# Feed-forward products of a four-layer trunk: each 128-row product issued as two 64-row products into two PSUM banks

## The chip, the cores and the metric

One core of a Trainium2 chip runs the whole program. The metric is device time in microseconds (us), median over runs. The kernel before was run twice: 3420.98 and 3409.43 us, median 3415.2 us. TensorE's clock has two levels, 1.2 and 2.4 GHz; the profile's granted clock is a share of the upper one (1.00 is 2.4 GHz).

## The reference, cut to what matters

256 latent tokens and 256 context tokens, 1024 channels, four layers. Each layer has a mixer (even layers: RWKV-7 time mixing and neighbourhood attention; odd layers: gated DeltaNet and an S5 state space model), an output projection, and a SwiGLU channel mixer with 2816 hidden channels, which is the part that changes:

```python
def swiglu(h, w_gate, w_up, w_down):
    return (jax.nn.silu(h @ w_gate) * (h @ w_up)) @ w_down

h_lat = h_lat + m_l[5] * swiglu(modulate(rmsnorm(h_lat, norm_ffn[l]), m_l[3], m_l[4]), f_gate[l], f_up[l], f_down[l])
if ctx_out:      # all layers but the last: the context tokens too
    h_ctx = h_ctx + m_c[5] * swiglu(...)
```

## The kernel before

Activations are channel-major: a tile `hT` of [128 partitions, 8 channel tiles, 512 tokens]. Every large fp32 product is made of three fp32r products, since both operands are split into a high and a low part: wh·xh, wh·xl, wl·xh (lines 222, 223 and 224 of `gemm`).

`unit` brings a piece of a weight matrix, 512 columns of 128 partitions (256 KB): a DMA on SP's queue (line 187, tile `w`, three buffers), a cast on ScalarE into `wh` (line 190) and a subtraction on VectorE into `wl` (line 191); `wh` and `wl` have three buffers each. In the feed-forward part a unit holds two channel tiles k of 256 output columns, so it feeds 2 x 2 x 3 = 12 matmuls. `gemm` takes 256 output columns at a time, in two PSUM banks, one for each 128 columns; the bank pairs alternate between tags "g" (tiles `pg` and `ph`) and "b" (two `pb` tiles), so one pair fills while the other is read.

`ffn` (line 355) first makes the modulated norm `nh`, `nl` (`norm_mod`, lines 322 to 326), channel tile by channel tile. It then runs over hidden blocks of 6, 6, 6 and 4 column tiles. For two column tiles at a time it computes the gate (`gate`: ScalarE reads the bank through Silu, line 370, into `sg`) and the up product (`up`: VectorE multiplies bank and `sg`, line 376; ScalarE and VectorE split the result into `gh` and `gl`, lines 377 and 378). After a block, the down product over its 6 or 4 channel tiles is added to `hT` (`add_h`, line 335, one VectorE instruction for each half of 256 tokens and each bank). Layers 0 to 2 work on 512 tokens, layer 3 on the 256 latent ones. In layers 0 and 2 `step()` also prepares the weights of the next S5 model (tiles whose names begin with `s5`), mostly on VectorE; these are the lines 1442 to 1640.

The program is written as Python code, but a scheduler sets the order on each engine, by a timeline that it models itself. Each engine then runs its own fixed order, and waits at an instruction until what it needs is there. So how many S5 instructions VectorE has to get through before a given `wl` is a matter of that order.

## Time and profile before

| what | value |
|---|---|
| median of the two runs | 3415.2 us (3409.43 to 3420.98) |
| span of the profiled execution | 3398.9 us |
| TensorE matmuls (PE) busy | 3120.2 us, 92% |
| weight loads (PEld) busy | 2418.1 us, 71% |
| VectorE (DVE) busy | 1920.1 us, 56% |
| ScalarE (ACT) busy | 1291.6 us, 38% |
| the four feed-forward stretches, together | 1351 us of the span |

PE stands for TensorE's matmuls, PEld for its weight loads, DVE for VectorE, ACT for ScalarE and SP for the queue that issues DMAs. The ends of matmuls are modelled, so the pace of matmuls is read from the distance of their starts, not from their durations. L222 is line 222 of the kernel. A group of instructions is written out<-in with the tiles' names, and the number in brackets behind a wait is its length with the one that ended it.

### The profile page before, as it was taken

Reading aid. Unit: us, or ns where it says so; the run is one execution under the profiler, and the core shown is the slowest. Engines: PE = TensorE matmul, PEld = TensorE weight load, DVE = VectorE, ACT = ScalarE, POOL = GpSimd, SP = SyncE. Lnnn points to the kernel's source line nnn. Section 1 sums busy time; section 2 is a strip of 40 time slices with the busy share of each in tenths; the row PEclk is TensorE's granted clock in tenths of the full one; section 3 lists DMA queues with packets and bytes.
Section 4 is the critical chain, followed back from the end, with each engine's and each line's share of the span. In section 5 each row is a group of like instructions: output and inputs, shape, how many; then the busy total and the mean of one; then the engine's idle time right before and its main releaser. Section 6 shows DMA issues by size and latency. Waiting matters only on the chain. (4 is left out here: it accounts for less than half of the span.)

```text
span 3398.9 us, 63286 instructions
## 1 busy us (share of the span) xinstructions
PE 3120.2 (92%) x24452; PEld 2418.1 (71%) x24452; DVE 1920.1 (56%) x4229; ACT 1291.6 (38%) x2785; POOL 515.4 (15%) x1159
## 2 busy tenths in 40 slices
PE   7999789999999889899999998877999999977998
PEld 4876456787787667578887776545787777756997
DVE  3556545766436696343434556555676445685554
ACT  3334344332235335232223333434333224534444
POOL 0223310000001653000000123220000000563000
PEclk8998889999999899899998998889999999978999
DMA  8635655345345544733336634553334334644554
GB/s 282 178 97 130 151 141 156 87 136 143 111 125 143 167 126 144 245 119 94 96 100 191 184 103 128 126 125 101 102 127 136 111 113 145 196 156 156 160 176 134
DMA packets 549696, 479.21 MB, mean 141 GB/s; under 512 B 176533, under 2 KB 480531, under 8 KB 549395
## 3 DMA queue, kind: packets, MB, share of 16 engines
q1 hardware_dynamic: 549394, 475.17, 48.5%
q8 instruction: 193, 3.16, 0.4%
q14 instruction: 109, 0.89, 0.1%
HBM read 406.34 MB, written 72.90 MB: 141 GB/s over the span
## 5 line engine op out<-in xcount | busy, mean ns | idle before, releaser
L191 DVE TENSOR_TENSOR wl<-w,wh 128x512 fp32r<-128x512 f32 x786 | 545.8, 697 | 766.4 <-ACT wh L190 746.6
L190 ACT CAST wh<-w 128x512 fp32r<-128x512 f32 x786 | 484.5, 619 | 1159.7 <-PE pb L223 343.3
L222 PE MATMUL pg<-nh,wh 128*128 128x512 f32 (+2 forms) x760 | 294.6, 388 | 19.4 <-ACT nh L270 8.7
L222 PE MATMUL pb<-nh,wh 128*128 128x512 f32 (+1 forms) x832 | 305.3, 374 | 4.0 <-ACT nh L325 2.7
L223 PE MATMUL pb<-nl,wh 128*128 128x512 f32 (+1 forms) x832 | 306.5, 371 | 0.0
L224 PE MATMUL pb<-nh,wl 128*128 128x512 f32 (+1 forms) x832 | 299.8, 373 | 0.0
L223 PE MATMUL pg<-nl,wh 128*128 128x512 f32 (+2 forms) x760 | 291.4, 383 | 0.6 <-DVE gr L1179 0.6
L224 PE MATMUL pg<-nh,wl 128*128 128x512 f32 (+2 forms) x760 | 290.4, 382 | 0.1
L298 POOL TENSOR_TENSOR nr<-nv,cst_base 128x4 f32<-128x4 f32 (+1 forms) x9 | 8.4, 938 | 1660.8 <-DVE nv L296 1660.8
L222 PE MATMUL ph<-nh,wh 128*128 128x512 f32 (+1 forms) x624 | 242.0, 388 | 10.1 <-ACT nh L325 5.9
L224 PE MATMUL ph<-nh,wl 128*128 128x512 f32 (+1 forms) x624 | 240.1, 385 | 0.0
L223 PE MATMUL ph<-nl,wh 128*128 128x512 f32 (+1 forms) x624 | 239.5, 384 | 0.0
L165 PE MATMUL px<-mw,cnd 128*32 128x256 f32 x1536 | 158.8, 450 | 83.5 <-DMA mw<-in_mod_w_dram 68.9
L222 PEld LDWEIGHTS pg<-nh,wh 128*128 128x128 f32 (+1 forms) x760 | 146.3, 193 | 56.4 <-ACT nh L270 11.3
L222 PEld LDWEIGHTS pb<-nh,wh 128*128 128x128 f32 x832 | 158.6, 192 | 36.3 <-ACT nh L325 3.2
L223 PEld LDWEIGHTS pb<-nl,wh 128*128 128x128 f32 x832 | 159.5, 192 | 29.3 <-DVE nl L271 1.3
L224 PEld LDWEIGHTS pb<-nh,wl 128*128 128x128 f32 x832 | 155.5, 191 | 30.7 <-issue 1.0
L223 PEld LDWEIGHTS pg<-nl,wh 128*128 128x128 f32 (+1 forms) x760 | 146.1, 192 | 34.8 <-issue 3.0
L224 PEld LDWEIGHTS pg<-nh,wl 128*128 128x128 f32 (+1 forms) x760 | 145.7, 192 | 29.1 <-issue 1.0
L858 POOL TENSOR_TENSOR Etmp<-E 64x14 f32<-64x14 f32 (+13 forms) x448 | 160.6, 359 | 31.1
L860 POOL TENSOR_TENSOR E<-E,Etmp 64x14 f32<-64x14 f32 (+13 forms) x448 | 158.8, 354 | 32.9
L222 PEld LDWEIGHTS ph<-nh,wh 128*128 128x128 f32 x624 | 119.6, 192 | 39.7 <-ACT nh L325 6.7
(578 smaller groups left out, 6440.8 us busy)
## 6 DMA issues: line engine op xcount, KB each, us to landing
mw<-in_mod_w_dram SPq DMA_DIRECT2D x192, 512.0 KB
w<-in_f_gate_dram SPq DMA_DIRECT2D x176, 256.0 KB
w<-in_f_up_dram SPq DMA_DIRECT2D x176, 256.0 KB
w<-in_f_down_dram SPq DMA_DIRECT2D x176, 256.0 KB
w<-in_w_in_even_dram SPq DMA_DIRECT2D x104, 256.0 KB
w<-in_w_in_odd_dram SPq DMA_DIRECT2D x80, 256.0 KB
w<-in_w_out_dram SPq DMA_DIRECT2D x64, 256.0 KB
hd<-hT SPq DMA_DIRECT2D x32, 256.0 KB
```

The lines of the kernel that those rows point to most:

```text
L165: nc.tensor.matmul(p[32 * c:32 * c + 32, :256], self.cnd[:, k, :], wt[:, 256 * c:256 * c + 256], start=k == 0, stop=k == KT - 1, skip_grou ...
L190: nc.scalar.copy(wh[:, :n], w[:, :n])
L191: nc.vector.tensor_tensor(wl[:, :n], w[:, :n], wh[:, :n].bitcast(F32), op=ALU.subtract)
L222: nc.tensor.matmul(o, wh[:, kk, m:m + mm], xh[:, k, tok], start=i == 0, stop=False)
L223: nc.tensor.matmul(o, wh[:, kk, m:m + mm], xl[:, k, tok], start=False, stop=False)
L224: nc.tensor.matmul(o, wl[:, kk, m:m + mm], xh[:, k, tok], start=False, stop=i == kt - 1)
L298: nc.gpsimd.tensor_tensor(r, v, self.mhalf[:, :nt], op=ALU.pow)
L858: nc.gpsimd.tensor_tensor(o, E[:, :s, s:s + 1].to_broadcast([m8, s, v]), E[:, s:s + 1, s + 1:].to_broadcast([m8, s, v]), op=ALU.mult)
L860: nc.gpsimd.tensor_tensor(E[:, :s, s + 1:], E[:, :s, s + 1:], o, op=ALU.add)
```

## The change

Each product of the feed-forward part is issued as two matmuls, one over partitions 0 to 63 and one over partitions 64 to 127, each into a PSUM bank of its own; whoever reads the result adds the two banks. `gemm_rows` takes 128 output columns at a time, in a pair of banks, and a unit of weights holds four channel tiles of 128 columns instead of two of 256. The gate now takes a copy on ScalarE, an addition on VectorE and the Silu on ScalarE; the up product takes a copy on ScalarE, an addition and a multiplication on VectorE before the split; `add_h` runs twice for each column tile.

```diff
+    def gemm_rows(self, W, kt, c0, cols, xh, xl, tok, done):
+        nc = self.nc
+        nt = tok.stop - tok.start
+        halves = (slice(0, 64), slice(64, 128))
+        ku = UNIT // 128
+        for m in range(cols // 128):
+            self.ngemm += 1
+            tag = "gb"[self.ngemm % 2]
+            ps = [self.bank(tag)[:, :nt] for _ in halves]
+            for k0 in range(0, kt, ku):
+                kn = min(ku, kt - k0)
+                wh, wl = self.unit(W[:, k0:k0 + kn, c0 + 128 * m:c0 + 128 * m + 128], kn, 128)
+                for kk in range(kn):
+                    k = k0 + kk
+                    for i, (w, x) in enumerate(((wh, xh), (wh, xl), (wl, xh))):
+                        for r, p in zip(halves, ps):
+                            nc.tensor.matmul(p, w[r, kk, :], x[r, k, tok], start=k == 0 and i == 0,
+                                             stop=k == kt - 1 and i == 2)
+            done(m, *ps)
...
-                def gate(m, p):
+                def gate(m, p, q):
                     s = fp.tile([128, NT], F32, name="sg", bufs=3)[:, :n]
-                    nc.scalar.activation(s, p, AF.Silu)
+                    nc.scalar.copy(s, p)
+                    nc.vector.tensor_tensor(s, s, q, op=ALU.add)
+                    nc.scalar.activation(s, s, AF.Silu)
                     gs.append(s)
 
-                def up(m, p):
+                def up(m, p, q):
                     s = gs[m]
                     i = 2 * u + m
-                    nc.vector.tensor_tensor(s, s, p, op=ALU.mult)
+                    t = self.tmp.tile([128, NT], F32, name="nt")[:, :n]
+                    nc.scalar.copy(t, p)
+                    nc.vector.tensor_tensor(t, t, q, op=ALU.add)
+                    nc.vector.tensor_tensor(s, s, t, op=ALU.mult)
                     nc.scalar.copy(gh[:, i, tok], s)
                     nc.vector.tensor_tensor(gl[:, i, tok], s, gh[:, i, tok].bitcast(F32), op=ALU.subtract)
...
-                self.gemm(Wg, KT, c0, 256, nh, nl, tok, gate)
-                self.gemm(Wu, KT, c0, 256, nh, nl, tok, up)
+                self.gemm_rows(Wg, KT, c0, 256, nh, nl, tok, gate)
+                self.gemm_rows(Wu, KT, c0, 256, nh, nl, tok, up)
                 step()
-            self.gemm(Wd[:, b0:b0 + nb, :], nb, 0, D, gh, gl, tok, lambda k, p: self.add_h(l, 40, k, p, tok))
+
+            def down(k, p, q):
+                self.add_h(l, 40, k, p, tok)
+                self.add_h(l, 40, k, q, tok)
+            self.gemm_rows(Wd[:, b0:b0 + nb, :], nb, 0, D, gh, gl, tok, down)
```

Line numbers of the changed kernel: the two matmuls stand on line 247, gate on 393 to 395, up on 402 to 406, `add_h` on 358; lines from 250 on have moved by 23, those behind `ffn` by 32 (L1606 of the change is L1574 of before).

The scheduler's order moves at more places than the diff shows. On TensorE, at the start of layer 0's feed-forward part, before (names: `pb` banks, `nh` and `nl` operands, `s5ct` an S5 transpose):

```order
L222 MATMUL pb<-nh,wh 128x512 x2
L1546 MATMUL pf<-cst_base,s5ct 128x128
L223 MATMUL pb<-nl,wh 128x512
L224 MATMUL pb<-nh,wl 128x512
L223 MATMUL pb<-nl,wh 128x512
L224 MATMUL pb<-nh,wl 128x512
L222 MATMUL pb<-nh,wh 128x512 x2
```

The same place of the change:

```order
L247 MATMUL pb<-nh,wh 128x512 x2
L247 MATMUL ph<-nh,wh 128x512
L247 MATMUL pg<-nh,wh 128x512
L1578 MATMUL pf<-cst_base,s5ct 128x128
L247 MATMUL pb<-nl,wh 128x512 x2
L247 MATMUL pb<-nh,wl 128x512 x2
L247 MATMUL pb<-nh,wh 128x512 x2
L247 MATMUL ph<-nl,wh 128x512
L247 MATMUL pg<-nl,wh 128x512
L247 MATMUL ph<-nh,wl 128x512
L247 MATMUL pg<-nh,wl 128x512
```

Every product is now a pair with the same operands and two banks (`pb` twice, or `ph` and `pg`), and two column tiles are begun side by side. Of the 6336 pairs 6256 stand side by side, and at 81 places something other than a pair stands between two of them.

On VectorE, later in the same part of layer 0, where the chain of the S5 powers ends with L1574 (L1606 of the change). Before, the last eleven rows up to it and the `wl` behind it:

```order
L191 TENSOR_TENSOR wl<-w,wh 128x512
L1572 TENSOR_TENSOR s5X<-s5t_7013,s5t_7014 128x32
L1567 TENSOR_TENSOR s5t_7013<-s5X 128x32
L1568 TENSOR_TENSOR s5t_7014<-s5X 128x32
L1569 TENSOR_TENSOR s5X<-s5t_7013,s5t_7014 128x32
L1570 TENSOR_TENSOR s5t_7013<-s5X 128x32
L1571 TENSOR_TENSOR s5t_7014<-s5X 128x32
L1573 COPY s5X<-s5X 128x8x32
L1572 TENSOR_TENSOR s5X<-s5t_7013,s5t_7014 128x32
L1574 TENSOR_SCALAR s5X<-s5X 128x8x32
L191 TENSOR_TENSOR wl<-w,wh 128x512
```

The change, around the same instruction:

```order
L1604 TENSOR_TENSOR s5X<-s5t_7123,s5t_7124 128x32
L1599 TENSOR_TENSOR s5t_7123<-s5X 128x32
L1600 TENSOR_TENSOR s5t_7124<-s5X 128x32
L1601 TENSOR_TENSOR s5X<-s5t_7123,s5t_7124 128x32
L1602 TENSOR_TENSOR s5t_7123<-s5X 128x32
L1603 TENSOR_TENSOR s5t_7124<-s5X 128x32
L1605 COPY s5X<-s5X 128x8x32
L1604 TENSOR_TENSOR s5X<-s5t_7123,s5t_7124 128x32
L1606 TENSOR_SCALAR s5X<-s5X 128x8x32
L191 TENSOR_TENSOR wl<-w,wh 128x512
L1615 TENSOR_TENSOR s5X<-s5cc,s5pout 128x576
L1618 TENSOR_TENSOR s5X<-s5cc,s5pout 128x576
```

The chain is the same; what has moved is the subtractions L191. Counted from the last `nl` of the norm, 19 of them stand ahead of L1574 before, with 149 S5 instructions; in the change 4 stand ahead of L1606, with 144 S5 instructions and two additions of the gate, and the L191 in the rows above is the fifth behind the last `nl` and the sixth of the layer. In layer 2 the order is the same.

On ScalarE, in the steady part (names: `sg` the gate, `nt` the copy of the first bank), before:

```order
L370 ACTIVATE sg<-pg 128x512
L190 CAST wh<-w 128x512
L370 ACTIVATE sg<-ph 128x512
L190 CAST wh<-w 128x512 x4
L377 CAST gh<-sg 128x512 x2
L190 CAST wh<-w 128x512 x3
```

and in the change:

```order
L190 CAST wh<-w 128x512 x2
L393 COPY sg<-pb 128x512
L395 ACTIVATE sg<-sg 128x512
L190 CAST wh<-w 128x512 x2
L402 COPY nt<-pg 128x512
L405 CAST gh<-sg 128x512
L190 CAST wh<-w 128x512 x2
```

Two casts of weights alternate with the two instructions that read a column tile, and the second of these waits for VectorE's additions in between.

## Rows read from the trace of the kernel before

**Rows 1.** The page: span, and busy time of each engine.
```profile
span 3398.9 us, 63286 instructions
PE 3120.2 (92%) x24452; PEld 2418.1 (71%) x24452; DVE 1920.1 (56%) x4229; ACT 1291.6 (38%) x2785; POOL 515.4 (15%) x1159
```
**Rows 2.** Busy time by stretch, the four feed-forward parts, layers 0 to 3.
```profile
core 0: us, PE busy (x) PEld busy (x) DVE busy (x) ACT busy (x) POOL busy (x), PEclk, DMA share, GB/s
630.00:1015.00 385.00, 383.86 (x1929) 308.14 (x1927) 229.56 (x494) 122.00 (x214) 0.00 (x0) 1.00 0.42 125
1450.00:1828.00 378.00, 378.00 (x1679) 302.40 (x1677) 148.68 (x254) 112.55 (x191) 0.00 (x0) 1.00 0.35 107
2438.00:2820.00 382.00, 381.28 (x1917) 305.97 (x1916) 225.48 (x480) 120.82 (x212) 0.00 (x0) 1.00 0.42 124
3178.00:3384.00 206.00, 199.42 (x1605) 193.00 (x1604) 119.25 (x216) 98.42 (x188) 0.00 (x0) 0.98 0.54 162
```
**Rows 3.** Timeline, gate and up of layer 1: start us, us, engine, line, instruction.
```profile
1509.54 0.39 PE L223 MATMUL pb<-nl,wh 128*128 128x512 f32 x1
1509.54 0.19 PEld L224 LDWEIGHTS pb<-nh,wl 128*128 128x128 f32 x1
...
1516.77 0.40 PE L224 MATMUL pb<-nh,wl 128*128 128x512 f32 x1
```
**Rows 4.** Timeline, TensorE, down of layer 1.
```profile
1517.70 0.39 PE L222 MATMUL ph<-gh,wh 128*128 128x512 f32 x1
...
1522.24 0.39 PE L224 MATMUL ph<-gh,wl 128*128 128x512 f32 x1
```
**Rows 5.** Timeline, TensorE: L674's 64-row pairs and what follows; L1609's full ones.
```profile
120.04 0.50 PE L674 MATMUL pf<-ar,bk 64*128 64x128 f32 x6
120.60 0.39 PE L674 MATMUL pf<-ar,bk 64*128 64x128 f32 x4
120.92 0.39 PE L244 MATMUL pg<-wl,nh 128*128 128x256 f32 x1
...
679.15 0.60 PE L1609 MATMUL pf<-cst_base,s5wt 128*128 128x128 f32 x4
```
**Rows 6.** Single lines: count, duration ns min/median/max, first and last start.
```profile
L376 DVE TENSOR_TENSOR sg<-sg,pb x44: 676/687/690, 1471.7 to 2791.9; 128x512 f32<-128x512 f32 x44
L370 ACT ACTIVATE sg<-pg x22: 597/598/602, 1462.2 to 2780.0; 128x512 f32<-128x512 f32 x22
L335 DVE SCALAR_TENSOR_TENSOR hT<-pb,mod,hT x140: 471/476/485, 577.4 to 3379.5; 128x256 f32<-128x256 f32 x140
L376 DVE TENSOR_TENSOR sg<-sg,pg x11: 410/413/415, 3191.6 to 3366.9; 128x256 f32<-128x256 f32 x11
L370 ACT ACTIVATE sg<-pb x22: 377/378/387, 3186.6 to 3361.4; 128x256 f32<-128x256 f32 x22
```
**Rows 7.** Last nl of layer 0's norm, and L1574's starts.
```profile
635.45 0.48 DVE L326 SCALAR_TENSOR_TENSOR nl<-nt,mod,nh 128x256 fp32r<-128x256 f32 x1
...
L1574 DVE TENSOR_SCALAR s5X<-s5X x2: 286/290/295, 688.9 to 2495.0; 128x256 f32<-128x256 f32 x2
```
**Rows 8.** Busy time between the two: all engines; VectorE's on wl; VectorE's on sg.
```profile
635.93:689.20 53.27, 53.27 (x238) 42.82 (x237) 47.85 (x176) 19.65 (x35) 0.00 (x0) 1.00 0.36 108
...
635.93:689.20 53.27, 13.05 (x19) 1.00 0.36 108
...
635.93:689.20 53.27, 5.21 (x8) 1.00 0.36 108
```
**Rows 9.** TensorE during that norm: us, busy (count), clock, DMA.
```profile
619.00:635.93 16.93, 15.77 (x61) 0.82 0.22 55
```
**Rows 10.** Layer 3: one unit's DMA, its cast, ScalarE's waits (total, times, longest).
```profile
3242.04 0.37 SPq L187 DMA_DIRECT2D w<-in_f_gate_dram  x1
...
3245.05 0.62 ACT L190 CAST wh<-w 128x512 fp32r<-128x512 f32 x1 [0.44 <-DMA w<-in_f_gate_dram]
...
ACT wh L190 <- DMA w<-in_f_up_dram: 25.4, 26, 2.1
```

## The prediction

> **What bounds the kernel now.** The page comes first: TensorE's matmuls are busy for 92% of the span, VectorE for 56%, ScalarE for 38% [rows 1]. Shares are means over unlike stages, so the second view is busy time by stretch, for the four feed-forward parts alone [rows 2]: in layers 0 to 2 TensorE is busy 383.86 of 385.00, 378.00 of 378.00 and 381.28 of 382.00 us at a granted clock of 1.00. There is no idle time for a reader or a load to give back; the only thing to gain is the pace of the products, and whatever holds TensorE up is added in full. VectorE has 149 of 378 us in layer 1 but 230 and 225 in layers 0 and 2, where the S5 preparation adds 81 and 77 us. Layer 3 has TensorE at 199.42 of 206.00 us.
>
> The third view is the timeline, for the pace. In gate and up 31 products lie between the two starts, 1509.54 and 1516.77: 233 ns each [rows 3]; in down 20 lie between 1517.70 and 1522.24: 227 ns [rows 4]. If a column takes one clock at 2.4 GHz, which is my estimate and fits these rows, 512 columns are 213 ns, and 14 to 20 ns a product are something else. Each weight load starts with the product ahead of it and takes 0.19 us [rows 3]: it is hidden already.
>
> **The change, part by part.** The sum is made against the profiled span, 3398.9 us; the median of the runs shown is 16.3 us above it, and I add that at the end.
>
> *Pace of the pairs.* The feed-forward parts hold 4 x 3 x 528 = 6336 products (22 x 8 each for gate, up and down, three matmuls each), 4752 of 512 columns and 1584 of 256. Each becomes a pair over the two halves of the partitions. The nearest rows are the pairs of L674, also 64 rows and 128 output columns into two banks, though plain fp32 and 128 columns wide: the pair at 120.04 and that at 120.60 are five pairs apart, 112 ns a pair [rows 5]. Full products of the same type and width, L1609, take (0.60 - 0.27) / 3 = 109 ns each, 0.27 being the modelled length of the last [rows 5]. So a pair costs what one costs, and 3 ns: 6336 x 3 = 19 us. Bounds: no pair beats its streaming, which for the 512-column ones is (231 - 213) x 4752 = 86 us of gain, and about 104 with the narrow ones at 118 against 107 ns (118 is an estimate: half of 233 is 117, and layer 3's 199.42 us over 1605 matmuls, waits included, are 124 [rows 2]); above, two products one behind the other, which is a rival.
>
> *Changes of form on TensorE.* At 81 places something else stands between two pairs. In the rows the last pair of L674 starts at 120.60 + 0.112 = 120.71 and the full product behind it at 120.92 [rows 5], 0.21 us later, 0.09 more than a pair's own step. In and out, at 81 places, that is 15 us; S5 products of narrow shape paid some of it before. I take 10, with 0 and 20 as ends.
>
> *The order on VectorE at the start of layers 0 and 2.* This is the largest term, and the diff does not show it. The last `nl` of layer 0's norm ends at 635.93 and L1574 ends at 689.2 [rows 7]. Between them VectorE works 47.85 us, 13.05 of it on nineteen L191 and 5.21 on the gate's readers [rows 8], so 47.85 - 13.05 - 5.21 = 29.6 us are 149 S5 instructions. In the change 144 of these stand ahead of the sixth `wl` of the layer, with four L191 and two additions between. The five left out are some of 0.7 us each, so 29.6 - 3.5 + 6 x 0.69 = 30 us have to pass on VectorE behind the last `nl` before the sixth `wl` is even begun, or 31 when it is done (an L191 takes 13.05 / 19 = 0.69 [rows 8], an addition out of a bank as much [rows 6]). Until then TensorE can finish five units, 60 pairs. Before, it had done about 55 products by the end of the norm (61 matmuls in that stretch, a few of them S5 transposes [rows 9]) and does 31 / 0.233 = 133 more in the next 31 us. The change is behind by 188 - 62 = 126 products, or 29 us; a part of the 81 us of S5 work on VectorE is then done earlier, but TensorE never had room to regain it. I take 28 for each of the two layers, 56 together; from 14 (if the chain is run through in half the time) to 35 (if the two additions, which wait for their tile's products, hold the queue, and the idle stretches bring the slow clock that the norm shows with 0.82 [rows 9]).
>
> *The readers in layers 0 to 2.* Gate: a copy of 0.60, an addition of 0.69 and a Silu of 0.60 us in the place of a Silu; up: a copy and an addition more; down: two L335 of 0.48 us more for each column tile [rows 6]. On VectorE that is 44 x 0.69 + 32 x 2 x 0.476 = 61 us a layer, and 12 further loads of weights (the six channel tiles of a down block need two units for 128 columns, 16 in the place of 12 units for a block) 8 us: layer 0 has 299 of 385 us, layer 1 218. A column tile is 24 pairs, 5.6 us, and its banks must be free one tile later; the chain copy, addition, multiplication, two L191 takes 0.60 + 2 x 0.69 + 2 x 0.69 = 3.4 us. It is covered by the other pair of banks, and costs nothing as long as it is. What is left uncovered is the tail of a block, where down waits for the last up tile's longer chain, 0.60 + 0.69 = 1.3 us more, at twelve blocks of these layers: 15 us at most. I take 10; from 0 to 40, if some tiles also lose their cover.
>
> *Layer 3.* Here a tile lasts only 24 x 0.118 = 2.8 us. A unit's cast starts 3.01 us after its DMA is issued [rows 10]; with the cast of 0.62 and an L191 of 0.69 [rows 8] a buffer of three goes round in 4.3 us, 1.44 a unit, against 12 x 0.118 = 1.42 for TensorE: ScalarE already waits for these DMAs, 25.4 us for one of the three matrices alone [rows 10]. The change puts into ScalarE's queue, behind every two casts, a copy and a Silu or split with VectorE's additions between: 0.38 + 0.41 + 0.38 = 1.2 us for gate, 1.6 for up [rows 6]. Two tiles then need a round of the buffer, a cast and this gap, 4.3 + 0.62 + 1.2 to 1.6, so 3.05 to 3.25 us a tile: 44 x 0.3 = 13 us. In down a tile of six channel tiles takes 18 x 0.118 = 2.1 us but two units, near 2.7 us: 24 x 0.6 = 14 us. I take 25, from 0 (the loads run ahead) to 50. The same bytes arrive in runs half as long; one round longer by 0.3 us would add 6 us, inside that range.
>
> *Sum.* 19 + 10 + 56 + 10 + 25 = 120 us: 3398.9 + 120 + 16.3 = 3535 us. The order in the three later mixers changes too, with the same work; I have no row for it, take 0, and leave 20 us to both sides.
>
> **The rivals.** *The pairs do not overlap.* The rows that show overlap are plain fp32, and at 112 ns for 128 columns they stream at half the rate of the fp32r products (233 ns for 512) [rows 3, 5]. If fp32r halves ran one behind the other, the cost would be 4752 x 0.231 + 1584 x 0.118 = 1285 us, all the other terms would be hidden behind it: 4700 us. Against it speaks that L674 uses the same halves and two banks in the same way. Chance 0.08.
>
> *The readers become the bound.* With 299 of 385 us VectorE has slack on the mean, but in 635.93 to 689.20 it was at 47.85 of 53.27 before anything was added [rows 8]. It decides if a tile's readers wait more than 2.2 us (5.6 less 3.4) behind S5 work, in about half the tiles of layers 0 and 2; 44 tiles a layer at 0.7 us are 60 us more: 3595 us. Chance 0.15. The Trainium skill, "TensorEngine Tiling (Array Packing)", section "PSUM Bottleneck", warns of this: tiling speeds up TensorE but not the evacuation of PSUM. In layer 1 the trace leaves 160 us of VectorE free after the change, so there it would not bind.
>
> *The order costs little.* If the five units ahead of the sixth `wl` are fewer than TensorE finds to do, or the S5 chain runs faster in one piece, and layer 3's loads run ahead, 19 + 10 + 10 remain: 3415 + 39 = 3454 us, no change by measure. Chance 0.15.
>
> *A pair is faster than one product.* If the 14 to 20 ns beyond streaming are what the switch of weights costs, and the other half's load and stream cover it, a pair comes at 213 ns. The gain of 104 us and the loss of 19 not paid leave 120 - 19 - 104 = -3: 3412 us, not slower. It decides from about 8 ns of gain a pair (120 - 19 - 6336 x 0.008 = 50 us, under 2%). For it speaks the excess in rows 3 and 4; against it, that L674 shows none. Chance 0.09. The Trainium skill, "TensorE: Matmul & The Clock Gate", section "What overlaps and what doesn't" in Part 3, says that a weight load overlaps running matmuls only when the row group differs, which would make this change a gain. The trace disagrees for the full products: a load of 0.19 us starts with the product ahead of it, and products still follow at 233 ns.
>
> **How the numbers follow.** Forecast 0.53 for 3535 us. A measurement of this kernel tells a change from none at about 2%, 68 us, so from 3347 to 3483. Slower: nearly all of the forecast (0.45 of 0.53), the readers 0.15, no overlap 0.08: 0.68. Same: the rest of the forecast 0.08, the cheap order 0.14, the faster pair 0.07: 0.29. Faster: 0.03, where a faster pair meets a cheap order. The range from 3440 to 3610 leaves out the pairs without overlap, most of the faster pair, and the tails.
>
> **What the profile of the change would show.** Pairs: two starts a few ns apart, the next pair 230 to 240 ns on; 460 would mean no overlap, 215 the gain. Order: behind the last `nl` of layers 0 and 2 TensorE idle in pieces of 5 to 10 us, waiting for `wl` L191, over by 35 us behind the norm. Readers: TensorE waiting for the release of a bank in the middle of layers 0 and 2 would make them the bound. Layer 3: 206 us become about 230, with TensorE waiting for the cast. Layer 1 should stay at 378 us and some 5 to 10. The prediction is wrong if layer 1, where no S5 work stands in the way, is longer by more than 20 us.

## The result, and the profile after

The change is slower: 3675.2 us (median of two runs, 3674.27 and 3676.05) against 3415.2 us, a ratio of 1.0744 with a 95% interval from 1.0706 to 1.0781. The direction was forecast, the size was not: 3535 us with a range to 3610. The profiled execution spans 3672.5 us, 273.6 more than that of before, where the sum had 120.

The page of the change, which answers [rows 1]:

```profile
span 3672.5 us, 77115 instructions
...
PE 3242.4 (88%) x30788; PEld 2524.8 (69%) x30788; DVE 2121.4 (58%) x4677; ACT 1386.2 (38%) x3009; POOL 517.5 (14%) x1159
```

TensorE, which had next to no idle time in layers 0 to 2 [rows 2], now has. For the comparison each feed-forward part is cut in the same way in all kernels, from the first `nl` of its norm to the last addition to `hT`; this begins 2 to 14 us earlier than the stretches of [rows 2]. The change, busy time by stretch, layers 0 to 3:

```profile
core 0: us, PE busy (x) PEld busy (x) DVE busy (x) ACT busy (x) POOL busy (x), PEclk, DMA share, GB/s
634.30:1112.90 478.60, 429.12 (x3551) 359.82 (x3551) 296.55 (x649) 153.59 (x285) 0.00 (x0) 0.93 0.36 102
1560.80:1946.80 386.00, 383.66 (x3256) 304.35 (x3256) 209.49 (x391) 141.97 (x254) 0.00 (x0) 0.99 0.34 99
2563.20:3039.10 475.90, 426.31 (x3551) 352.53 (x3551) 296.42 (x648) 153.51 (x286) 0.00 (x0) 0.94 0.36 102
3405.00:3658.20 253.20, 224.55 (x3196) 206.75 (x3196) 154.32 (x307) 113.98 (x245) 0.00 (x0) 0.97 0.46 132
```

The kernel before in the same cut:

```profile
620.50:1014.40 393.90, 392.76 (x1955) 314.52 (x1955) 238.48 (x529) 127.68 (x229) 0.00 (x0) 0.99 0.41 122
1443.50:1827.50 384.00, 383.15 (x1701) 305.32 (x1702) 154.66 (x271) 115.28 (x199) 0.00 (x0) 0.99 0.36 108
2424.50:2819.00 394.50, 393.78 (x1954) 315.06 (x1954) 238.10 (x530) 127.43 (x229) 0.00 (x0) 0.99 0.41 122
3176.30:3383.40 207.10, 200.57 (x1607) 194.21 (x1607) 120.83 (x219) 98.60 (x189) 0.00 (x0) 0.98 0.53 161
```

Layer 1, where no S5 work stands in the way, takes 2 us more; some 4 us of other products have left it, as shown below under the mixers, so the change itself costs it about 6. Layers 0 and 2 take 85 and 81 more, layer 3 takes 46 more. What lies between these stretches (mixers and output projections, here called mixers 0 to 3) takes 2064 us in place of 2004, though the change does not touch it.

That layer 1 is nearly unchanged is the pace. The change, timeline of TensorE in layer 1's gate and up:

```profile
1614.72 0.39 PE L247 MATMUL pg<-nh,wl 64*128 64x512 f32 x1
1614.72 0.40 PE L247 MATMUL ph<-nl,wh 64*128 64x512 f32 x1
1614.95 0.40 PE L247 MATMUL pg<-nh,wh 64*128 64x512 f32 x1
...
1617.75 0.40 PE L247 MATMUL pb<-nh,wh 64*128 64x512 f32 x1
```

Two halves start in the same 10 ns, and from 1614.72 to 1617.75 there are 13 steps: 233 ns a pair, where [rows 3] had 233 ns a product. The pairs overlap fully, and at this pace they cost nothing. They bring nothing either: a pair takes as long as the full product did.

Where layer 0 loses its time (the change, busy time of TensorE in five of its stretches; `PEclk` is the granted clock):

```profile
635.00:667.00 32.00, 21.47 (x119) 0.71 0.09 23
667.00:699.00 32.00, 21.34 (x126) 0.79 0.26 76
855.00:893.00 38.00, 32.01 (x284) 0.87 0.42 107
953.00:1013.00 60.00, 45.53 (x376) 0.86 0.44 110
1083.00:1113.00 30.00, 24.76 (x176) 0.94 0.47 137
```

Busy time multiplied by the granted clock is an estimate of the work at the full clock. By it the first two rows lose 64 - (21.47 x 0.71 + 21.34 x 0.79) = 32 us, 21 of them idle and the rest at the lower clock, and the other three 10, 21 and 7, together 38. The first two are the stall that was forecast. The other three were not foreseen.

### The profile page after: what moved, and what is told of

It reads as the page before. It is cut to its first block, busy times and chain, and to the rows that moved or that the text cites. A ratio compares the mean times of both kernels' runs of the same rounds, so it can differ in the third digit from the quotient of the medians.

```text
span 3672.5 us, 77115 instructions
## 1 busy us (share of the span) xinstructions
PE 3242.4 (88%) x30788; PEld 2524.8 (69%) x30788; DVE 2121.4 (58%) x4677; ACT 1386.2 (38%) x3009; POOL 517.5 (14%) x1159
## 5 line engine op out<-in xcount | busy, mean ns | idle before, releaser
L191 DVE TENSOR_TENSOR wl<-w,wh 128x512 fp32r<-128x512 f32 (+1 forms) x834 | 549.0, 662 | 737.0 <-ACT wh L190 703.2
L190 ACT CAST wh<-w 128x512 fp32r<-128x512 f32 (+1 forms) x834 | 490.2, 593 | 1016.8 <-PE pb L247 198.2
L247 PE MATMUL pb<-nh,wh 64*128 64x512 f32 (+1 forms) x1408 | 320.0, 374 | 30.8 <-DVE sg L394 16.7
L247 PE MATMUL pb<-nl,wh 64*128 64x512 f32 (+1 forms) x1408 | 316.2, 373 | 1.8 <-DVE nl L349 1.5
L247 PE MATMUL pb<-nh,wl 64*128 64x512 f32 (+1 forms) x1408 | 313.3, 372 | 4.2 <-DVE wl L191 4.0
L247 PE MATMUL ph<-nh,wh 64*128 64x512 f32 (+1 forms) x704 | 263.6, 374 | 18.0 <-DVE sg L394 8.6
L247 PE MATMUL pg<-nh,wh 64*128 64x512 f32 (+1 forms) x704 | 263.7, 375 | 12.5 <-DVE sg L394 8.8
L247 PE MATMUL ph<-nh,wl 64*128 64x512 f32 (+1 forms) x704 | 262.2, 372 | 2.5 <-DVE wl L191 2.4
L247 PE MATMUL pg<-nl,wh 64*128 64x512 f32 (+1 forms) x704 | 262.2, 372 | 2.2 <-DVE nl L349 2.2
L247 PE MATMUL ph<-nl,wh 64*128 64x512 f32 (+1 forms) x704 | 263.7, 375 | 0.0
L165 PE MATMUL px<-mw,cnd 128*32 128x256 f32 x1536 | 161.8, 470 | 108.4 <-DMA mw<-in_mod_w_dram 107.8
```

The lines of the kernel that those rows point to most:

```text
L165: nc.tensor.matmul(p[32 * c:32 * c + 32, :256], self.cnd[:, k, :], wt[:, 256 * c:256 * c + 256], start=k == 0, stop=k == KT - 1, skip_grou ...
L190: nc.scalar.copy(wh[:, :n], w[:, :n])
L191: nc.vector.tensor_tensor(wl[:, :n], w[:, :n], wh[:, :n].bitcast(F32), op=ALU.subtract)
L247: nc.tensor.matmul(p, w[r, kk, :], x[r, k, tok], start=k == 0 and i == 0, stop=k == kt - 1 and i == 2)
```

## The experiments

All lengths are in us and in the cut above; M0 to M3 are mixers 0 to 3, F0 to F3 the feed-forward parts of layers 0 to 3. "Beside" is the kernel before in the same series. Before and the change are medians of two runs, before_raw4 and before_raw4_pool of five and four; every other time is a single execution. The kernel before came at 3405.9 to 3430.8 in these series, so a difference of 20 us between two totals says little. The lengths are firmer: F0 is 393.9 to 394.8 in the five executions that leave layer 0 and its stores as they were. The lengths of before_raw4 are of its fastest execution, 3390.7 us.

| kernel | M0 | F0 | M1 | F1 | M2 | F2 | M3 | F3 | time | beside |
|---|---|---|---|---|---|---|---|---|---|---|
| before | 620.5 | 393.9 | 429.1 | 384.0 | 597.0 | 394.5 | 357.3 | 207.1 | 3415.2 | |
| before_again | 623.1 | 394.4 | 435.5 | 384.0 | 593.2 | 393.1 | 358.9 | 209.1 | 3407.9 | 3410.4 |
| the change | 634.3 | 478.6 | 447.9 | 386.0 | 616.4 | 475.9 | 365.9 | 253.2 | 3675.2 | 3415.2 |
| after_again | 630.8 | 481.9 | 437.0 | 385.9 | 611.2 | 474.2 | 365.3 | 250.6 | 3653.4 | 3430.8 |
| two_full | 619.0 | 406.8 | 436.5 | 419.5 | 604.9 | 409.0 | 366.8 | 226.7 | 3505.4 | 3410.4 |
| units_only | 622.6 | 403.6 | 448.1 | 415.9 | 586.0 | 404.0 | 362.7 | 226.7 | 3486.9 | 3405.9 |
| s5_pool | 630.5 | 455.3 | 446.1 | 386.2 | 608.8 | 449.6 | 363.2 | 250.8 | 3606.8 | 3410.4 |
| s5_behind | 654.9 | 377.1 | 576.9 | 389.1 | 605.2 | 377.1 | 500.2 | 257.7 | 3754.3 | 3410.4 |
| paced | 657.4 | 380.7 | 536.1 | 385.9 | 604.8 | 380.7 | 468.9 | 259.1 | 3689.9 | 3405.9 |
| same_order | 655.3 | 428.8 | 449.6 | 385.7 | 616.9 | 426.3 | 360.3 | 254.0 | 3593.2 | 3420.3 |
| same_order_raw4 | 639.1 | 428.3 | 447.7 | 389.5 | 616.1 | 430.2 | 363.0 | 215.6 | 3546.1 | 3420.3 |
| odd_pairs | 624.9 | 394.1 | 435.8 | 386.0 | 615.5 | 394.6 | 362.6 | 259.3 | 3489.2 | 3405.9 |
| l0_pairs | 631.1 | 477.1 | 436.8 | 382.3 | 574.7 | 394.2 | 366.6 | 206.2 | 3486.2 | 3430.8 |
| l2_pairs | 621.2 | 394.7 | 434.3 | 383.1 | 596.3 | 475.9 | 360.0 | 204.8 | 3487.1 | 3430.8 |
| raw4 | 640.6 | 469.2 | 444.1 | 387.5 | 599.7 | 465.3 | 359.1 | 217.1 | 3599.0 | 3405.9 |
| two_full_raw4 | 623.7 | 404.8 | 451.6 | 422.6 | 582.7 | 404.5 | 358.2 | 198.9 | 3463.1 | 3430.8 |
| before_raw4 | 621.0 | 394.8 | 439.1 | 384.3 | 590.7 | 394.2 | 360.6 | 189.4 | 3405.4 | 3420.3 |
| before_raw4_pool | 624.0 | 390.6 | 445.2 | 383.2 | 594.9 | 389.8 | 359.3 | 187.4 | 3390.6 | 3420.3 |

### Is it the pairs, or what comes with them

**two_full** keeps units, banks and readers of the change and takes the pairs away: full products, the first half of the channel tiles into one bank, the second into the other.

```diff
-                    for i, (w, x) in enumerate(((wh, xh), (wh, xl), (wl, xh))):
-                        for r, p in zip(halves, ps):
-                            nc.tensor.matmul(p, w[r, kk, :], x[r, k, tok], ...
+                    p, f = ps[2 * k // kt], (0, kt // 2)
+                    for i, (w, x) in enumerate(((wh, xh), (wh, xl), (wl, xh))):
+                        nc.tensor.matmul(p, w[:, kk, :], x[:, k, tok], start=k in f and i == 0, ...
```

> The change with full 128-row products: the first half of the channel tiles k goes into one bank and the second half into the other, so units of weights, banks and readers are those of the change and only the pairs are gone. The scheduler's own order comes out like that of before (4, 5, 2 S5 instructions between loads of weights on VectorE in place of 18, 50, 30). Theory A (the loss in layers 0 and 2 is the order that follows from the pairs): layers 0 and 2 at 395 to 405 us, layer 1 at 384 to 388, layer 3 still 245 to 255, total near 3675 - 2 x 77 = 3520. Rival B (the readers and the smaller units are the bound in layers 0 and 2, in whatever order): layers 0 and 2 at 455 to 480, total 3640 to 3680.

3505.4 us: some 170 of the change's 260 us are gone with the pairs (some 150 against after_again), and theory A's layers 0 and 2 came, nearly. Units, banks and readers being the same, what comes with the pairs is what costs most, and the order is the larger part of it, as the runs below show. Two_full changes one thing more: its first bank is complete half a tile before the second, where the two banks of a pair end together, so its readers have more time. That the scheduler counts the two halves of a pair one behind the other, and so sees twice the time on TensorE that there is, would explain such orders; it is inferred from them and was not shown. Layer 1 missed (419.5 for 384 to 388): the order puts more adaLN products there, those that make each layer's modulation from the conditioning (L165). TensorE on L165 within that part of two_full (stretch, length, matmuls, loads, clock, DMA):

```profile
1462.30:1881.80 419.50, 35.45 (x256) 8.97 (x251) 0.99 0.43 126
```

In before this part has 72 of them, busy for 8.02 us, so they account for 27 of the 36 us over its 384.0. Layer 3 is 227, not 245 to 255, so the pairs have a part of that loss too.

**units_only** also takes the second bank and the adding readers away and keeps only the 128-column units.

```diff
-            ps = [self.bank(tag)[:, :nt] for _ in halves]
+            p = self.bank(tag)[:, :nt]
...
-            done(m, *ps)
+            done(m, p)
```

> Full products into one bank with the readers of before, but the 128-column units of the change (four channel tiles of 128 columns, so half as long runs in DRAM and sixteen units in the place of twelve for a down block of six). With full products, two banks and the adding readers layer 3 took 227 us against 209 of before. If the units make those 18 us, layer 3 is 220 to 228 here; if the readers make them, 207 to 212. Layers 0 and 2: 393 to 400. Total 3410 to 3450, and more only if the order puts adaLN products into layer 1.

Layer 3 is 226.7, the same as with the readers: in full products the units make the whole loss there, the readers none. In layers 0, 1 and 2 the readers (two_full less units_only) cost 3, 4 and 5 us, the units 9 and 11 in layers 0 and 2. Layers 0 and 2, 403.6 and 404.0, are above their 393 to 400. The total, 3486.9, misses the 3410 to 3450 by the same move of adaLN products into layer 1 (415.9), which the expectation named as its exception.

### Layers 0 and 2

**s5_pool** moves the stores of the prepared S5 weights from SP's queue to GpSimd's.

```diff
-            nc.sync.dma_start(zd[c], zs[32 * c:32 * c + 16])
+            nc.gpsimd.dma_start(zd[c], zs[32 * c:32 * c + 16])
...
-                nc.sync.dma_start(self.t[qt][16 * s:16 * s + 16, b],
+                nc.gpsimd.dma_start(self.t[qt][16 * s:16 * s + 16, b],
```

and likewise those of `self.x` and `self.w`. What it aims at is this stretch of SP's queue in the change (start, length in us, issues):

```profile
842.20 14.37 SPq L187 DMA_DIRECT2D w<-in_f_down_dram  x6
860.84 1.73 SPq L1675 DMA_DIRECT2D s5zd<-s5zs  x4
862.78 1.20 SPq L1651 DMA_DIRECT2D s5xd<-s5X  x2
864.15 10.93 SPq L1678 DMA_DIRECT2D s5td<-s5zd  x16
875.18 1.59 SPq L187 DMA_DIRECT2D w<-in_f_down_dram  x3
```

No weights are issued from 856.57 to 875.18. First SP waits for `s5zs`, which comes late, then it issues sixteen small stores for 10.93 us. In this time TensorE uses up what the three buffers hold; the cast waits up to 13.4 us. The change, ScalarE's wait in layer 0 (total, times, longest):

```profile
ACT wh L190 <- DMA w<-in_f_down_dram: 39.7, 8, 13.4
```

> The change, with the four kinds of DMA that store the prepared S5 weights (lines 1642 to 1678) issued on GpSimd's queue in place of SP's. VectorE's order at the start of layers 0 and 2 is the same as in the change. Theory A: of the 85 and 81 us lost in layers 0 and 2 some 30 are VectorE's order at the start, and 35 to 40 are weight loads that stand on SP behind sixteen S5 issues of 10.9 us; these go, so layers 0 and 2 take 435 to 447 us, layer 1 386 and layer 3 253 as before this edit, total 3595 to 3615. Rival B: the loss later in these layers is VectorE and ScalarE, which the edit does not touch: 470 to 480 us and 3665 to 3680 in all.

Theory A is nearer, with less than it said: F0 455.3 and F2 449.6, 23 and 26 us less, above its 435 to 447. The total, 3606.8, is inside its range only because the mixers are 16 us shorter too, which the edit was not meant to bring. The same wait in s5_pool:

```profile
ACT wh L190 <- DMA w<-in_f_down_dram: 7.3, 3, 2.9
```

**s5_behind** holds all S5 preparation of a layer back until its last `add_h`.

```diff
-                n.ffn(l, tok, f, step)
-                for _ in prep:
-                    pass
+                end = n.ffn(l, tok, f, lambda: None)
+                with tc.issue_after(end):
+                    for _ in prep:
+                        pass
```

> The change, with the S5 preparation of layers 0 and 2 held back until the last addition to the residual stream of that layer, so that no S5 instruction stands in the feed-forward part. Theory A: layers 0 and 2 then take 384 to 390 us like layer 1, and the 81 us of S5 work on VectorE come behind, partly beside the next mixer: total between 3675 - 2 x 90 = 3495 and 3660. Rival B (the pairs and readers themselves cost something in these layers): 410 us and more even without S5 work.

F0 and F2 are 377.1, below the 393.9 of before and even the 384 of layer 1. Layer 0 in s5_behind and in paced, the next kernel:

```profile
654.90:1032.00 377.10, 372.88 (x3172) 314.36 (x3172) 209.69 (x390) 139.83 (x254) 0.00 (x0) 0.99 0.34 98
657.40:1038.10 380.70, 375.14 (x3172) 313.45 (x3172) 244.64 (x595) 139.81 (x254) 0.00 (x0) 0.99 0.34 99
```

The S5 matmuls are gone from it too: 3172 stand here, 4 more than the pairs' own 3168, where before has 371 more than its own 1584. So 377.1 is not to be set against 393.9. At 233 ns in gate and up and at the 227 ns of [rows 4] in down the 1584 pairs take 366 us, an estimate; the norm, the units and the readers have the other 11. With no S5 work among them the pairs lose next to nothing. The total misses upward, 3754.3: M1 and M3 are 141 us longer, since the S5 work then stands where nothing covers it. TensorE's longest waits in M1 of s5_behind are for it:

```profile
PE pf L1642 <- DVE s5X L1602: 26.9, 4, 23.7
PE pf L1666 <- DVE s5X L1618: 26.6, 7, 13.3
```

**paced** takes s5_pool and ties each S5 instruction of VectorE behind one of the layer's `wl`, evenly.

```diff
+                work = [i for i in list(todo)[k0:] if i.engine == n.subs[0].engine]
+                for j, i in enumerate(work):
+                    tc.add_manual_dep(i, n.subs[4 + j * 92 // len(work)].name, ...)
```

> The change with the S5 stores on GpSimd's queue, and each of the S5 instructions of VectorE tied in order behind one of the layer's loads of weights wl, evenly over the 5th to the 97th, so that at most four stand between two wl. Pairs, units and readers stay. Theory A (the rest of the loss in layers 0 and 2, 455 and 450 us with the S5 stores moved, is VectorE's order): 388 to 402 us for both, total near 3607 - 2 x 57 = 3493, to 3540 where S5 work is left for the next mixer. Rival B (VectorE with readers and S5 work together is the bound): 425 us and more for these layers.

F0 and F2 are 380.7, better than expected, but the total is 3689.9: most of the S5 work slid into M1 and M3, which are 100 and 110 us longer than before_again's. By the rows above VectorE does 35 us of it in layer 0 (244.64 less 209.69), where the change does 87 (296.55 less 209.69), and TensorE none. The run shows that this much S5 work on VectorE need not stall the pairs. It does not show that all of it fits.

**same_order** ties the S5 instructions behind those `wl` behind which they stand in two_full (a table, `AHEAD`, counted from the layer's last `wl`), with a high priority, so that nearly all of them stay in the layer. The edit against paced:

```diff
-                    tc.add_manual_dep(i, n.subs[4 + j * 92 // len(work)].name, ...)
+                    ahead = AHEAD[j * len(AHEAD) // len(work)]
+                    tc.add_manual_dep(i, n.subs[max(len(n.subs) - ahead - 1, 0)].name, ...)
```

> The change with the S5 stores on GpSimd's queue and VectorE's S5 instructions tied behind those loads of weights wl behind which they stand in the kernel with full products and the same units and readers (the one that took 3505 us). Pairs, units and readers are untouched; only the order is borrowed. Theory A (pairs cost nothing beyond the orders that come with them): first mixer and layer 0 together 1025 to 1040 us (1113 in the change, 1026 in the kernel with full products), layer 2 at 395 to 412, layer 3 still 250 to 258, total 3500 to 3535. Rival B (64-row pairs, with S5 work in between, lose time on TensorE whatever the order): together 1070 or more, total 3590 and more.

A miss. F0 and F2 are 428.8 and 426.3: 27 and 23 us less than s5_pool's, but 22 and 17 more than two_full's, and the total of 3593.2 is where rival B had put it. Layer 0 in two_full and in same_order:

```profile
619.00:1025.80 406.80, 402.31 (x1967) 316.90 (x1967) 289.22 (x649) 155.33 (x285) 0.00 (x0) 0.99 0.42 119
655.30:1084.10 428.80, 419.38 (x3551) 324.16 (x3550) 291.99 (x638) 154.77 (x285) 55.73 (x104) 0.98 0.40 113
```

The borrowed order took most of the idle time away: 9.4 us are left, where the change has 49.5 and two_full 4.5. The other 17 us are busy time of TensorE for the same products, a part of it at the lower clock. Another part is what rival B says, that pairs with S5 work in between lose time on TensorE whatever the order. Four S5 products between two products of the layer, before and in the change:

```profile
688.19 0.40 PE L222 MATMUL pg<-nh,wh 128*128 128x512 f32 x1
688.43 0.60 PE L1609 MATMUL pf<-cst_base,s5wt 128*128 128x128 f32 x4
688.78 0.48 PE L223 MATMUL pg<-nl,wh 128*128 128x512 f32 x1
...
708.15 0.39 PE L247 MATMUL pb<-nh,wh 64*128 64x512 f32 x1
708.47 0.66 PE L1641 MATMUL pf<-cst_base,s5wt 128*128 128x128 f32 x4
709.06 0.49 PE L247 MATMUL pb<-nh,wh 64*128 64x512 f32 x1
```

From one product of the layer to the next it is 0.59 us before and 0.91 in the change: 0.32 us more to go from 64-row products to 128-row ones and back. Measured in the same way, at a granted clock of 1.00, single S5 transposes (L1546, L1578 in the change) take 0.26 and 0.58, the groups of eight products of the next norm (L284, L307) 1.03 and 1.30. The S5 products of L1633 (L1665 in the change) have 64 rows themselves and show none of it: 64 of them take 1.69 us in both kernels. Layer 0 of the change has 25 such places, some 8 us, and that of same_order 29, some 9 us of its 22. These sums are estimates. How the rest parts into clock, idle time and the readers' shorter time stays open, since the order of TensorE, ScalarE and SP was not borrowed.

M0 is 655 us, 25 more than in s5_pool. It is 655 and 657 in s5_behind and paced too, and in these three kernels the scheduler has put M0's own instructions into another order: on TensorE some 3050 of 5550 stand at another place, where s5_pool has the change's order.

**same_order_raw4**, the same with four buffers for raw weights.

> The same with four buffers for raw weights. Theory A: layer 3 goes from 255 to 217 us, as it did in the change with four buffers, the rest within 10 us: 3465 to 3500. Rival: the fourth buffer gave its gain in the change by another order on SP, and here layer 3 stays above 240.

Layer 3 came as expected (215.6), the total did not (3546.1), by what same_order had missed.

### Layer 3

**raw4** gives the change a fourth buffer for raw weights.

```diff
-        self.raw = pool("raw", 3)
+        self.raw = pool("raw", 4)
```

> The change with four buffers for raw weights in place of three. Theory A: in layer 3 the round of three buffers (4.3 us for three units) limits, so four bring layer 3 from 253 to 235 us or less, and in layers 0 and 2 the fourth covers part of the 11 us in which SP issues S5 stores: 10 to 20 us less in each; total 3610 to 3640. Rival B (layer 3 is held by ScalarE's casts standing behind a copy that waits, an order, not by the number of buffers): layer 3 at 248 or more.

F3 falls from 253 to 217, more than expected; F0 and F2 by 9 and 11; the total is 3599.0, below the 3610 to 3640. **before_raw4** is the same edit on the kernel before, in three rounds.

> The kernel before with four buffers for raw weights. Layer 3 waits 70 us on ScalarE for transfers of weights there, but TensorE is busy 199 of 206 us: if the buffers limit only the pair kernel's layer 3 and not this one, it gives 0 to 8 us, 3400 to 3410; if orders in the mixers shift with it, within 20 us either way.

The total came (3405.4), the reason did not: F3 is 189.4 in place of 207 to 209, more than the 0 to 8 us allowed. Busy time of layer 3 in before_raw4:

```profile
3184.70:3374.10 189.40, 189.40 (x1608) 189.38 (x1608) 121.63 (x219) 99.44 (x188) 0.00 (x0) 0.99 0.60 174
```

The same products that were busy for 200.57 us with three buffers are busy for 189.40 with four. In three rounds the ratio to before is 0.9948 (0.9924 to 0.9973), faster by half a per cent.

**two_full_raw4** parts the remaining difference of layer 3 with four buffers, 189 against 217.

> Full products with the units, banks and readers of the change, and four buffers for raw weights. Layer 3 took 227 us with three buffers; the change 253 with three and 217 with four, the kernel before 207 and 189. If the fourth buffer takes away all that the units cost, layer 3 is 187 to 195 here and the 28 us that the change keeps with four buffers belong to the pairs' order; if the units or readers still cost with four, 205 to 217.

198.9 lies between both expectations: 9.5 us stay with units and readers, 18 with the pairs. With three buffers, too, the pairs had their part, and it shows on ScalarE, whose queue also holds the casts. What it waits for in layer 3, the change (two lines) and two_full (one):

```profile
ACT gh L405 <- DVE sg L404: 28.3, 22, 1.4
ACT sg L395 <- DVE sg L394: 17.5, 21, 0.9
...
ACT gh L405 <- DVE sg L404: 4.0, 8, 0.8
```

The readers are the same instructions in both, yet ScalarE waits 46 us for VectorE's additions and multiplications with pairs and under 5 without.

### The mixers

**before_again** is the kernel before, unchanged.

> The kernel before, unchanged, to see how much a stretch varies from one chip to another. The first mixer (start to the first normalised tile of layer 0's feed-forward part) has the same instructions in the same order in both kernels, yet took 621 us before and 635 us in the change. If that drift belongs to the run or the chip, this kernel's first mixer lies anywhere from 621 to 635 us here and moves with the other kernels of this job. If the change itself causes it, this one takes 621 (within 3 us) while kernels with the change's products take 635 on the same chip. Feed-forward parts: 393, 384, 394 and 206 us, each within 3.

M0 is 623.1. **odd_pairs** has pairs in layers 1 and 3 only, **l0_pairs** in layer 0 only, **l2_pairs** in layer 2 only.

```diff
-                self.gemm(Wg, KT, c0, 256, nh, nl, tok, gate)
+                g = self.gemm_rows if l % 2 else self.gemm
+                g(Wg, KT, c0, 256, nh, nl, tok, gate)
```

with `up`, the readers and down alike, and `l == 0` or `l == 2` in the two others.

> Pairs, 128-column units and the adding readers in layers 1 and 3 only; layers 0 and 2 as before, and VectorE's order in them comes out as before. Theory A (pairs cost what full products cost; the losses are orders on the other engines): layer 0 and 2 at 393 to 396 us, layer 1 at 384 to 388, layer 3 at 250 to 256, the mixers within 10 us of before in sum, total 3410 + 2 + 45 = 3457 (3445 to 3470). Rival B (pairs anywhere in the program make the mixers slower too, as the first mixer's 631 to 634 us in the two kernels full of pairs against 619 to 623 in three others suggest): first mixer near 630 and total 3480 to 3500.

> Pairs, units and adding readers in layer 0 only. Theory A (each layer's pairs lengthen that layer and the mixer behind it, and layer 0's pairs also the first mixer): first mixer 630 to 640 us, layer 0 at 472 to 482, second mixer 443 to 450, then as before (layer 1 384, layer 2 394, layer 3 208); total 3408 + 84 + 12 + 12 = 3516 (3500 to 3530). Rival B (the first mixer's length belongs to the run, or to pairs in all layers): first mixer 619 to 625, total 3490 to 3505.

> Pairs, units and adding readers in layer 2 only. Theory A: first mixer 619 to 625 us, layer 0 at 394, second mixer 429 to 439, layer 1 at 384, third mixer 590 to 605, layer 2 at 470 to 480, fourth mixer 362 to 370, layer 3 at 208; total 3408 + 82 + 7 = 3497 (3480 to 3515). Rival B (pairs anywhere lengthen every mixer): first mixer 630 and more, total over 3520.

The layers came as theory A has them: with pairs F0 is 477.1 and F2 475.9, without 394; F1 is 386.0. The mixers behind them did not: M1 of l0_pairs is 436.8, not 443 to 450, and M3 of l2_pairs 360.0, not 362 to 370. The totals add up less well. odd_pairs is 3489.2, outside its 3445 to 3470, because M2 is 615.5. l0_pairs is 3486.2, below its 3500, because M2 is 574.7. Over all executions M2 is 600 to 617 in the nine with pairs in layer 1 and 575 to 605 in the nine without. So it goes with layer 1's pairs, with some 20 us from one kernel to the next that they do not explain. One thing that moves is adaLN work. L165 in layer 1, before:

```profile
1443.50:1827.50 384.00, 8.02 (x72) 2.25 (x72) 0.99 0.36 108
```

and in the change:

```profile
1560.80:1946.80 386.00, 4.29 (x32) 1.16 (x32) 0.99 0.34 99
```

Forty of these products have left layer 1; in the change M2 has 416 in place of 392 and M1 16 more, in odd_pairs M2 has all forty. In l0_pairs only 8 left layer 1 and M2 has 384, yet it is 20 us shorter, and raw4 has 433 with an M2 of 599.7; so their number alone does not explain M2, and its cause stays open.

**after_again** is the change, unchanged.

> The change unchanged, on the chip of the other three. Theory A: first mixer 630 to 638 us, the parts within 3 us of what they were (layers 478, 386, 476, 253), total 3665 to 3685. Rival: the first mixer's 634 us were of that one execution, and it comes at 619 to 625 here with a total near 3660.

The feed-forward parts came within 4 us and M0 is 630.8; M1 is 437.0 in place of 447.9. The total is 3653.4, below its 3665. M0 is 630 us or more in all eight kernels with pairs in layer 0 and 619 to 625 in all others, with and without four buffers. In l0_pairs and l2_pairs the instructions of M0 stand in the same order on every engine, and the difference of 10 us builds up in steps, nearly all of it before 260 us. So the 10 us come with layer 0's pairs, and their cause stays open. Of the eight, raw4, s5_behind, paced, same_order and same_order_raw4 have another order in M0 as well, so the comparison rests on the change, s5_pool and l0_pairs (630 to 634).

### A version faster than both

**before_raw4_pool** is before_raw4 with s5_pool's edit, in three rounds.

> The kernel before with four buffers for raw weights and the S5 stores on GpSimd's queue. Layers 0 and 2 lose about 1 us at one store burst and some 9 us against layer 1 in all: 0 to 10 us less for both together, on top of layer 3's 0 to 8; total 3390 to 3410. If GpSimd's issues delay its own work in the mixers, up to 15 us more than before.

3390.6 us (3388.64 to 3393.21) against 3420.3, a ratio of 0.9908 (0.9891 to 0.9925), inside the 3390 to 3410 expected. That is clear of the spread of the runs, but 0.9% is less than the 2% that the prediction asks of a change. Two of the things that held the change up, the three buffers and the stores on SP, cost the kernel before a little too: F0 and F2 are 390.6 and 389.8, F3 187.4.

## Why the prediction was wrong, step by step

The sum had 120 us; the pair of executions after_again and before_again differs by 245. Four steps failed: there is no term for SP's queue (it cost 50 us), layer 3 was taken as bound by TensorE (25 us in place of 42 to 46), the mixers were put at 0 without a row (34 to 60), and the smaller units were priced on VectorE alone (20 us in layers 0 and 2). The prediction's own sign of being wrong, layer 1 longer by more than 20 us, did not show: it tests the pairs, and they were right.

- **Pace of the pairs, 19 us: right in kind, 0 in size.** 233 ns a pair, and layer 1 at 386.0 against 384.0 with everything else in it, or about 6 us more when the adaLN products that left it are counted. The 3 ns were taken from 128-column plain fp32 pairs [rows 5]; for 512 columns nothing is left of them. The Trainium skill, "TensorE: Matmul & The Clock Gate", section "What overlaps and what doesn't" in Part 3, would have made different row groups the condition for hiding a weight load, and so the change a gain. Here the full products were at 233 ns, the pairs are at 233 ns.
- **Changes of form, 10 us: right in kind, about half.** A place costs 0.27 to 0.32 us where 128-row products stand between pairs, and not the 0.18 of L674's rows. Some 25 such places in layer 0 and as many in layer 2 make 8 us each, six in layer 1 and six in layer 3 under 2 us each: some 20 us, an estimate.
- **VectorE's order at the start, 28 us a layer: right.** The two stretches up to 699.00 lose 32 us in layer 0, the lower clock included, and tying S5 work to two_full's places gave 27 and 23 us a layer. (The 62 in the working should be the 60 of its own count of pairs; that is half a us.) The stall lasted 50 us and not 35, as the additions of L394 stand in the same queue: two of TensorE's three longest waits in layer 0 are for a bank that L394 has still to read, and both stand in these stretches. The change, TensorE's waits in layer 0:

```profile
PE pb L247 <- DVE sg L394: 8.6, 2, 8.0
PE pg L247 <- DVE sg L394: 6.8, 2, 5.9
```

- **What is missing from the sum: SP's queue, 23 to 26 us a layer.** The working looked for who waits on VectorE and never asked what stands on SP ahead of a `w`. The sixteen issues were there in the trace of before, as a burst of 10.91 us, and hidden. SP's queue in layer 0, before:

```profile
790.88 8.94 SPq L187 DMA_DIRECT2D w<-in_f_down_dram  x4
804.09 1.74 SPq L1643 DMA_DIRECT2D s5zd<-s5zs  x4
805.93 0.39 SPq L187 DMA_DIRECT2D w<-in_f_down_dram  x1
806.37 0.52 SPq L1619 DMA_DIRECT2D s5xd<-s5X  x1
807.14 10.91 SPq L1646 DMA_DIRECT2D s5td<-s5zd  x16
818.15 1.56 SPq L187 DMA_DIRECT2D w<-in_f_down_dram  x3
```

  Here one `w` goes out between SP's wait for `s5zs` and the burst, so the longest stretch without weights is 11.8 us; in the change none does, and it is 18.6. About 50 us in both layers were lost to this, by s5_pool. A down block's units, 512 and 256 columns by turns, may add to it, since they fill the three buffers with less work; that is argued, and units_only and two_full have the same units without such a loss.
- **Readers in layers 0 to 2, 10 us: right.** 3 to 5 us a layer by two_full less units_only. The rival that made them the bound (3595 us) came nearest to the total, by luck: with the same readers and full products F0 and F2 are 407 and 409, and with pairs and readers but little or no S5 work among them 381 and 377. The Trainium skill's warning, "TensorEngine Tiling (Array Packing)", section "PSUM Bottleneck", that evacuation does not speed up, is not what bound this kernel. Instead the 9 and 11 us of the smaller units, which the sum had as VectorE time only, are unpredicted. With these, layer 0 adds up to 32 + 23 + 8 + 9 + 3 = 75 of its 85 us; some 10 stay open.
- **Layer 3, 25 us: mis-sized, 42 to 46.** The round of the raw buffers was named, and a fourth buffer did give 36 us back. The failing step is to read 199.42 busy us of 206.00 [rows 2] as TensorE's need. The need was 189 or less, so the loads already set the pace, and each thing that lengthens their round counts in full: 18 us for the units (units_only), and the rest comes with the pairs, where ScalarE's casts stand behind 46 us of waits for VectorE's readers in place of 5. How much of those waits TensorE pays for is not shown.
- **The mixers, 0 with 20 to either side: wrong, 34 to 60.** 8 to 14 in M0, which goes with layer 0's pairs; 18 or 19 in M2, which goes with layer 1's; 6 to 9 in M3; M1 between 2 and 19, not the same in two executions of the change. The causes stay open. "The same work in another order" is not a reason for 0.
- **The range.** The terms of layers 0 and 2 were bounded each by itself, without one for a queue not looked at. In sum for one pair of executions (after_again less before_again, 245 us): F0 and F2 169, F3 42, F1 2, mixers 34.

## What to carry to other kernels

Where a scheduler sets the order, a change that doubles the number of instructions of one engine can change the order on all, as it did here; build the changed kernel and read the order of every queue that a critical buffer passes, the DMA queue included, not just that of the engine that looked busiest. A burst of DMA issues or a small number of buffers that is hidden today can fall due as soon as something else moves. Products of another shape between the new ones have a price of their own, so measure it at one such place. Ask for a spare buffer first: it is a one-line experiment, and here it took 18 us off a layer that looked bound by TensorE, and half a per cent off the kernel.

## What was not expected of the hardware

The two halves are not in lock-step. In the timeline of layer 1 above, `pg` stands at its product of `wl` while `ph` starts that of `nl`: one half runs a product ahead of the other, and keeps the distance over the rows shown. And the busy time of narrow products can hold waits, since the profile's ends of matmuls are modelled: the matmuls of layer 3, the same products, took 200.57 us of busy time with three buffers of weights and 189.40 with four, with a granted clock of 0.98 and 0.99. Last, going from 64-row products to 128-row ones and back took 0.27 to 0.32 us a place, and pairs alone pay none of it.
